# Reordering the first layer's projections, one exponential per group, and 64-column halves for the in-chunk products of a Mamba-2 + differential-attention trunk

## The chip, the cores and the metric

The kernel runs on one core of a Trainium2 chip, in one launch. A core has a matrix engine (TensorE, in the profile PE, with its weight loads apart as PEld), three engines for elementwise work (VectorE: DVE, ScalarE: ACT, GpSimd: POOL) and a queue engine (SyncE: SP) that starts transfers. Each engine takes its own instructions strictly in the order of its list and waits for the others by semaphores. The metric is the time of one execution on the device in microseconds (us); lower is better.

## The reference

Two layers over 512 tokens of width 1024. The first is a Mamba-2 layer with eight groups of four heads, the second differential attention against shared keys and values. Only the first layer is touched here:

```python
def ssd_chunked_scan(xdt, adt, bm, cm):
    def step(state, inp):
        x_c, a_c, b_c, c_c = inp
        acs = jnp.cumsum(a_c, axis=1)
        seg = acs[:, :, None] - acs[:, None, :]
        decay = jnp.exp(jnp.where(causal, seg, -jnp.inf))
        cb = jnp.einsum("blgn,bsgn->blsg", c_c, b_c)
        y_diag = jnp.einsum("blsgr,bsgrp->blgrp", cb[..., None] * decay, x_c)
        y_off = jnp.einsum("blgn,bgrpn->blgrp", c_c, state) * jnp.exp(acs)[..., None]
        to_end = jnp.exp(acs[:, -1:] - acs)
        new_state = (state * jnp.exp(acs[:, -1])[..., None, None]
                     + jnp.einsum("blgn,blgrp->bgrpn", b_c, x_c * to_end[..., None]))
        return new_state, y_diag + y_off
...
def mamba2_layer(x, ...):
    h = rms_norm(x, norm_g)
    zxbcdt = h @ w_in
    ...                                  # causal conv of width 4 and SiLU on x, B, C; softplus on dt
    y = ssd_chunked_scan(xs * dt[..., None], a * dt, bm, cm)
    y = y + d_skip.reshape(G, R, 1) * xs
    y = gated_group_rms_norm(y, z, gate_norm_g)   # y * silu(z), then RMS norm over each group's 256 channels
    return x + y @ w_out
```

After it come one shared key/value projection, the attention layer with its own projections, and a final RMS norm.

## The kernel before

All numbers are float32. Each weight matrix and each activation of a large product is split into a high part that the matrix engine multiplies at full speed and the low rest (`whi`/`wlo`, `a_hi`/`a_lo`, `yh`/`yl`); one product is then three matmuls (`mm3`, high-high, high-low, low-high). The small products of the scan are plain float32, and the matrix engine records two passes for each of them.

The first layer is cut into segments, each with two 1 MB weight blocks that are fetched and split ahead of use (ACT writes `whi`, DVE writes `wlo`; buffers for two blocks of each, so a block's `whi` can be written only when the block two before it has been multiplied for the last time):

- `z0` to `z3`: the gate projection for 512 channels, that is two groups; results leave PSUM through a SiLU on ACT (`z_out`, tile `zs`).
- `g0` to `g7`: a group's B, C and x columns (`pg`, 96 matmuls). Each of the four PSUM banks goes through the convolution (`conv`, tile `xc`): one multiply and three multiply-adds on DVE, two steps on ACT. The bank is free when the last multiply-add has read it.
- `o0` to `o3`: the output projection of two groups (`po`, 96 matmuls); DVE adds each bank to the residual `x_tok`. Segment `o3` needs `yh`/`yl` of groups 6 and 7; its second half is written apart (`last_rows`).

`order_a` sets the order of the segments. The projections form a stream (`stream_a`), and between them `ssd(g)` carries out the scan of group `g` in 128-token chunks: transposes (`pbt`, `pxt`), B·C products (`pcb`), dt-scaled x (`xdt`), the skip term (`dx`), states (`psA`, `psB`, `hst`), the in-chunk products (`pyd`: for each of four chunks and four heads, 128 weight columns of `dec` against 64 columns of `xdt`), the state's share (`po1`, `po2`, `tmp`), the gate, the group norm (`ss4`, `rsqrt`), and the transposition back (`pyt`) into `yh`/`yl`. Its tiles `xdt`, `dx`, `xe`, `hst` and `tmp` have one buffer each, so `ssd(g+1)` starts its `xdt` only when `ssd(g)` has read `dx` for the last time. `decays` fetches the cumulative decays (a broadcast DMA), subtracts and masks them on POOL and takes the exponentials on ACT. ACT loads a table each time it changes between SiLU and the exponential.

In this part the written order is not the order of execution on an engine. A scheduler that works ahead of time merges the stream and the scan into one fixed list for each engine. It chooses by its own estimate of times, and what it chose is seen below. From `last_rows` on the written order holds.

Of the kernel before, what the change touches and what calls it, by code (L numbers as in the profile page):

```python
# [17 lines left out]
P = 128  # L18
# [4 lines left out]
G = 8  # L23
R = 4
HD = 64
H = 32
NQ = 4
# [3 lines left out]
BIG = 1e30  # L31
# [6 lines left out]

C_GA, C_GK, C_GB, C_GG, C_SG, C_DTB, C_AL, C_CB, C_CW = 0, 8, 16, 24, 40, 41, 42, 43, 75
N_PAR = 203  # L40


class Ordered:
# [18 lines left out]
def trunk(ctx, tc, x, x_t, par, w_dt, w_in, w_out, w_kvqg, w_bo, d_skip, lam_qk, fin_g, out):  # L62
    nc = tc.nc
    V, A, T = (Ordered(tc, e) for e in (nc.vector, nc.scalar, nc.tensor))
    GP = nc.gpsimd
# [21 lines left out]

    order_a = "z0 g0 g1 z1 g2 g3 z2 g4 o0 g5 z3 g6 g7 o1 o2 o3".split()  # L90
    segs = []
    for it in order_a + ORDER_B:
        segs += [(it[0], int(it[1]) if len(it) == 2 else it, k) for k in range(2 if it[0] in "zgo" else 1)]
# [28 lines left out]
    def load(i):  # L122
# [8 lines left out]
        def split():  # L131

            pool, tags = (bp, ("dec", "dec")) if seg == ("o", 3, 1) else (wp, ("whi", "wlo"))
            hi, lo = (pool.tile([P, nk, w], F32R, tag=tag, name=f"{n}{i}", bufs=2) for n, tag in zip(("whi", "wlo"), tags))
# [207 lines left out]
    conv_out = {}  # L342

    def z_out(j, t, ps):
        zs = bp2.tile([P, 512], F32, tag="zs", name=f"zs{j}_{t}", bufs=6)
        A.activation(zs, ps, AF.Silu, scale=r_col[:, t:t + 1])
        zt[j, t] = zs

# [180 lines left out]
    bss = small.tile([P, 2, NT], F32, name="bss", bufs=1)  # L529
    decs = {}  # L530

    def decays(j):

        for g in (2 * j, 2 * j + 1):
            hs = slice(R * g, R * g + R)
            dec = bp.tile([P, R, NQ, P], F32, tag="dec", name=f"dec{g}", bufs=2)
            nc.sync.dma_start(dec.rearrange("p h c l -> p (h c l)"),
                                acs_d[hs].rearrange("h c l -> (h c l)").partition_broadcast(P))
            een = small.tile([P, R, 2], F32, tag="een", name=f"een{g}")
            GP.tensor_copy(een, dec[:, :, 1:3, P - 1])  # L540
            for h in range(R):
                GP.tensor_tensor(out=dec[:, h], in0=dec[:, h], in1=acs_tok[:, :, R * g + h].unsqueeze(2).to_broadcast([P, NQ, P]), op=ALU.subtract)
                GP.affine_select(out=dec[:, h], in_=dec[:, h], compare_op=ALU.is_ge, fill=-BIG, base=0,
                                 pattern=[[0, NQ], [1, P]], channel_multiplier=-1)
            decs[g] = (dec, een)
        for g in (2 * j, 2 * j + 1):
            dec, een = decs[g]
            A.activation(een, een, AF.Exp)
            for h in range(0, R, 2):
                A.activation(dec[:, h:h + 2], dec[:, h:h + 2], AF.Exp)  # L550

    def ssd(g):
        bc, cc, x0, x1 = conv_out.pop(g)
# [58 lines left out]
        T.matmul(po1[:, 256:512], lhsT=cc[:, P:2 * P], rhs=hsf[:, 0], start=True, stop=True)  # L612
# [1 line left out]
        for c in (2, 3):  # L614
# [5 lines left out]
        zo = (g % 2) * 256  # L620
        u = dx.rearrange("p c h e -> p c (h e)")
        tm = tmp.rearrange("p c h e -> p c (h e)")
        for c in range(NQ):
            if c:
                GP.tensor_tensor(out=u[:, c], in0=u[:, c], in1=tm[:, c], op=ALU.add)
            V.tensor_tensor(out=u[:, c], in0=u[:, c], in1=zt[g // 2, c][:, zo:zo + 256], op=ALU.mult)
# [492 lines left out]
```

## Time and profile before

| what | us |
|---|---|
| median of 3 runs | 737.5 (737.13 to 738.17) |
| the profiled execution's own time | 736.51 |
| its span, first to last instruction | 734.7 |
| PE busy, as the profile models it | 723.1 |
| PE weight loads (PEld) | 605.0 |
| DVE / ACT / POOL busy | 530.8 / 445.3 / 114.8 |
| ACT table loads, 33 of them | 42.3 |
| in-chunk products `pyd`, 256 passes, as records | 30.3 |

A row of a timeline in the next part reads: start in the span, duration of the run of like instructions, engine, line, operation, written tile <- read tiles, shape, count, and in brackets the engine's idle time before it and what ended it. Nearly all instructions of PE, DVE and ACT bear line 53, that of a helper, and are told apart by their tiles. A PE matmul record is longer than its share of the engine, because the next one starts before it ends: a record of 0.39 us is followed by the next 0.23 us after its start.

### The profile page before, as it was taken

What the parts mean: (1) busy time and instruction counts of PE and PEld (TensorE: products, weight loads), DVE (VectorE), ACT (ScalarE), POOL (GpSimd) and SP (SyncE); (2) the same over time, 40 slices, a digit from 0 to 9 for tenths busy, and PEclk for the clock granted to TensorE, in tenths of its full rate; (3) what the DMA queues carried; (4) which work ended last, traced back from release to release, by engine and by line L of the source; (5) the groups of instructions that cost most, each with busy time, mean ns of one, the idle gap of its engine ahead of it and who ended that gap; (6) DMA issues with size and microseconds to landing.
All of it is one profiled execution on the core that took longest, in us unless ns stands there. A gap on an engine that the chain in (4) does not pass through costs nothing.

```text
span 734.7 us, 10327 instructions
## 1 busy us (share of the span) xinstructions
PE 723.1 (98%) x3733; PEld 605.0 (82%) x3733; DVE 530.8 (72%) x1202; ACT 445.3 (61%) x975; POOL 114.8 (16%) x158
## 2 busy tenths in 40 slices
PE   9999999999999999999999999999999999999996
PEld 7788878888887888877888879888898898889874
DVE  5679955798568669469895655666757857785886
ACT  6849672864829356256433258766766766766566
POOL 0117231402233141150110201000000000000002
PEclk9999999999999999999999999999999999999999
DMA  8552313224132233132113220331221131122003
GB/s 314 215 193 97 128 45 116 78 95 172 59 114 65 108 115 116 58 116 102 71 58 114 87 86 8 115 115 58 65 109 57 58 116 58 58 80 93 29 1 114
DMA packets 12914, 70.83 MB, mean 96 GB/s; under 512 B 1728, under 2 KB 2496, under 8 KB 5312
## 3 DMA queue, kind: packets, MB, share of 16 engines
q1 hardware_dynamic: 12576, 69.90, 26.5%
q8 instruction: 29, 0.48, 0.3%
q10 hardware_dynamic: 288, 0.28, 0.1%
q14 instruction: 21, 0.17, 0.1%
HBM read 68.02 MB, written 2.16 MB: 96 GB/s over the span
## 4 chain that ended last, share of the span: by engine, by line
PE 86%; DVE 6%; ACT 5%; issue 1%; DMA 1%; POOL 0%; ACTq 0%; POOLq 0%; SPq 0%
PE pg L53 20%; PE po L53 13%; PE pz L53 10%; PE pt L53 7%; PE pv L53 6%; PE pq L53 6%; PE pk L53 6%; PE pyd L53 4%; PE pb L53 3%; PE sc L53 3%; PE pc L53 2%; DVE wlo L53 2%; ACT L53 1%; PE pyt L53 1%; PE pxt L53 1%
## 5 line engine op out<-in xcount | busy, mean ns | idle before, releaser
L53 DVE SCALAR_TENSOR_TENSOR wlo<-raw,prm,whi 128x512 fp32r<-128x512 f32 (+1 forms) x256 | 151.4, 640 | 49.6 <-ACT whi L53 49.2
L53 ACT ACTIVATE whi<-raw,prm 128x512 fp32r<-128x512 f32 (+1 forms) x256 | 137.1, 609 | 58.5 <-PE pz L53 12.4
L53 PE MATMUL pg<-a_hi,whi 128*128 128x512 f32 x256 | 102.4, 401 | 0.4 <-DVE xc L53 0.4
L53 PE MATMUL pg<-a_hi,wlo 128*128 128x512 f32 x256 | 102.7, 404 | 0.0
L53 PE MATMUL pg<-a_lo,whi 128*128 128x512 f32 x256 | 101.4, 397 | 0.0
L53 DVE SCALAR_TENSOR_TENSOR xc<-pg,prc,xc 128x511 f32<-128x511 f32 (+2 forms) x96 | 70.0, 743 | 4.4 <-ACT xc L53 3.6
L53 PEld LDWEIGHTS pg<-a_hi,whi 128*128 128x128 f32 x256 | 48.2, 188 | 11.4 <-issue 0.8
L53 PEld LDWEIGHTS pg<-a_hi,wlo 128*128 128x128 f32 x256 | 48.1, 188 | 11.0
L53 PEld LDWEIGHTS pg<-a_lo,whi 128*128 128x128 f32 x256 | 48.2, 188 | 10.8
L53 PE MATMUL po<-whi,yh 128*128 128x512 f32 x128 | 50.9, 400 | 0.7 <-ACT yh L53 0.6
L53 PE MATMUL po<-wlo,yh 128*128 128x512 f32 x128 | 50.9, 400 | 0.4 <-DVE wlo L53 0.4
L53 PE MATMUL pz<-wlo,a_hi 128*128 128x512 f32 x128 | 50.5, 401 | 0.0
L53 PE MATMUL pz<-whi,a_lo 128*128 128x512 f32 x128 | 50.1, 399 | 0.0
L53 PE MATMUL po<-whi,yl 128*128 128x512 f32 x128 | 49.9, 396 | 0.0
L53 PE MATMUL pz<-whi,a_hi 128*128 128x512 f32 x128 | 49.6, 400 | 0.0
L53 ACT ACT_TABLE_LOAD x33 | 42.3, 1283 | 9.5 <-DVE xc L53 7.9
L957 POOL TENSOR_TENSOR ot<-ot,fg 128x512 f32<-128x512 f32 x4 | 5.1, 1285 | 257.6 <-PE pc L53 256.4
L53 ACT ACTIVATE s<-s,mx 128x128 f32<-128x128 f32 (+3 forms) x64 | 35.6, 559 | 9.5 <-DVE mx L53 9.3
L580 POOL TENSOR_TENSOR xe<-xdt,tok 128x256 f32<-128x256 f32 x24 | 15.4, 672 | 152.5 <-DVE xdt L53 152.5
L53 DVE CUSTOM_DVE_ANT_0 s<-sc,bias 128x128 f32<-128x128 f32 (+3 forms) x64 | 29.4, 488 | 12.3 <-PE sc L53 11.9
L53 PE MATMUL pv<-whi,b_hi 128*128 128x256 f32 x128 | 36.6, 286 | 0.0
L53 ACT ACTIVATE tmp<-dx 128x256 f32<-128x256 f32 x32 | 13.1, 411 | 38.0 <-DVE dx L53 38.0
(244 smaller groups left out, 1749.1 us busy)
## 6 DMA issues: line engine op xcount, KB each, us to landing
raw<-in_w_in SPq DMA_DIRECT2D x23, 1024.0 KB, 4.9
raw<-in_w_kvqg SPq DMA_DIRECT2D x16, 1024.0 KB, 4.8
dec<-acs_d SPq DMA_DIRECT2D x8, 1024.0 KB, 4.8
raw<-in_w_out SPq DMA_DIRECT2D x8, 1024.0 KB, 4.7
raw<-in_w_bo SPq DMA_DIRECT2D x4, 1024.0 KB, 4.8
x_tok<-in_x SPq DMA_DIRECT2D x4, 512.0 KB, 9.4
out<-ot SPq DMA_DIRECT2D x7, 256.0 KB, 2.4
raw<-in_w_in SPq DMA_DIRECT2D x4, 256.0 KB, 5.4
```

The costliest lines, as they stand in the source:

```text
L53: i = op(*args, **kw)
L580: GP.tensor_tensor(out=xe[:, c], in0=xdt[:, c], in1=toe_tok[:, c, hs].unsqueeze(2).to_broadcast([P, R, HD]), op=ALU.mult)
L957: GP.tensor_tensor(out=o, in0=o, in1=f, op=ALU.mult)
```

## The change

Three things are changed.

1. `order_a`: `z0 g0 g1 z1 g2 g3 z2 g4 o0 g5 z3 g6 g7 o1 o2 o3` becomes `z0 g0 z1 g1 g2 z2 g3 o0 g4 z3 g5 o1 g6 g7 o2 o3`. To go with it, a gate tile is kept for each group (256 channels, 12 buffers) in place of one for two groups (512 channels, 6 buffers); its SiLU is two instructions in place of one.
2. `decays` is called for one group, two groups ahead, in place of two groups at once. The decays that `een` held lie behind `dec` in one tile of 2056 columns, and one exponential covers both in place of three.
3. Each product of `pyd` is done as two: weight columns 0 to 63 into PSUM partitions 0 to 63, and columns 64 to 127 into partitions 64 to 127.

```diff
+N_DEC = R * NQ * P + 2 * R
...
-    order_a = "z0 g0 g1 z1 g2 g3 z2 g4 o0 g5 z3 g6 g7 o1 o2 o3".split()
+    order_a = "z0 g0 z1 g1 g2 z2 g3 o0 g4 z3 g5 o1 g6 g7 o2 o3".split()
...
     def z_out(j, t, ps):
-        zs = bp2.tile([P, 512], F32, tag="zs", name=f"zs{j}_{t}", bufs=6)
-        A.activation(zs, ps, AF.Silu, scale=r_col[:, t:t + 1])
-        zt[j, t] = zs
+        for i in range(2):
+            zs = bp2.tile([P, 256], F32, tag="zs", name=f"zs{j}_{t}_{i}", bufs=12)
+            A.activation(zs, ps[:, i * 256:(i + 1) * 256], AF.Silu, scale=r_col[:, t:t + 1])
+            zt[2 * j + i, t] = zs
...
-    def decays(j):
-        for g in (2 * j, 2 * j + 1):
-            hs = slice(R * g, R * g + R)
-            dec = bp.tile([P, R, NQ, P], F32, tag="dec", name=f"dec{g}", bufs=2)
...
-        for g in (2 * j, 2 * j + 1):
-            dec, een = decs[g]
-            A.activation(een, een, AF.Exp)
-            for h in range(0, R, 2):
-                A.activation(dec[:, h:h + 2], dec[:, h:h + 2], AF.Exp)
+    def decays(g):
+        hs = slice(R * g, R * g + R)
+        both = bp.tile([P, N_DEC], F32, tag="dec", name=f"dec{g}", bufs=2)
+        dec = both[:, 0:R * NQ * P].rearrange("p (h c l) -> p h c l", h=R, c=NQ)
+        een = both[:, R * NQ * P:].rearrange("p (h q) -> p h q", h=R)
...
+        A.activation(both, both, AF.Exp)
+        decs[g] = (dec, een)
...
                     o = (c % 2) * 256 + h * HD
-                    T.matmul(pyd[q][:, o:o + HD], lhsT=dec[:, h, c, :], rhs=xdt[:, c, h, :], start=True, stop=True)
+                    for r in (slice(0, 64), slice(64, 128)):
+                        T.matmul(pyd[q][r, o:o + HD], lhsT=dec[:, h, c, r], rhs=xdt[:, c, h, :], start=True, stop=True)
...
-        if g % 2 and g < G - 1:
-            decays((g + 1) // 2)
+        if g < G - 2:
+            decays(g + 2)
...
     decays(0)
+    decays(1)
```

In `split`, the last block of `o3` borrows the two `dec` buffers; it now takes the first 2048 columns of the larger tile. `o3` and all that follows it are as before.

The lists that the scheduler makes of it differ from the first layer's beginning to its end. Three places count for the prediction. The first is PE at the end of the first layer, around the scan of group 7 (`pyd7`, `po17`, `po27`, `pyt7`) and the output projections `po2` and `po3`. Before, the second block of products stands inside `po2`, and 23 more matmuls of `po2` and the 24 of `po3` that need only group 6 follow ahead of `pyt7`:

```order
L53 MATMUL po2_1_1_3566<-whi29_3406,yl5_2664 128x512
L53 MATMUL po2_1_2_3580<-whi29_3406,yh4_2206 128x512
L53 MATMUL pyd7_1_3290<-xdt7_3243,dec7_2601 128x64 x8
L53 MATMUL po17_3300<-hst7_3267,xc31_3171 128x256
L53 MATMUL po27_3302<-hst7_3267,xc31_3171 128x256 x2
L53 MATMUL po2_1_2_3580<-wlo29_3407,yh4_2206 128x512
...
L53 MATMUL po3_0_3_3676<-whi30_3474,yl6_3068 128x512
L53 MATMUL pyt7_0_3338<-ident_74,tmp7_3279 128x128
...
L53 MATMUL po3_0_0_3628<-whi30_3474,yh7_3336 128x512
```

Now:

```order
L55 MATMUL po3_0_3_3812<-whi30_3474,yl6_3324 128x512
L55 MATMUL psA7_3524<-xe7_3515,bt7_3497 128x256 x2
L55 MATMUL psB7_3530<-xe7_3515,bt7_3497 128x256
L55 MATMUL pyd7_0_3536<-xdt7_3499,dec7_2840 64x64 x16
L55 MATMUL pyd7_1_3554<-xdt7_3499,dec7_2840 64x64 x16
L55 MATMUL po17_3572<-hst7_3523,xc31_3427 128x256
L55 MATMUL po27_3574<-hst7_3523,xc31_3427 128x256 x2
L55 MATMUL pyt7_0_3610<-ident_74,tmp7_3535 128x128
...
L55 MATMUL po3_0_0_3764<-whi30_3474,yh7_3608 128x512
```

What moved: all of `po2` and the part of `po3` that needs only group 6 now stand ahead of `psA7`; between `psA7` and `pyt7` no projection is left. The products are 64 by 64 and twice as many.

The second place is ACT just before that, between the scaling of group 6 (`tmp6`, the last reading of `dx6`) and the state of group 7. `whi32` is the first block of the next layer. It takes the buffer of `whi29`, which the last matmul of `po2` reads. Before:

```order
L53 ACTIVATE tmp6_3010<-dx6_2975,y_y_3051 128x256 x4
L53 CAST yh6_3067<-pyt6_0_3069 128x512
L53 CAST yh6_3067<-pyt6_1_3076 128x512
L53 COPY bt7_3241<-pbt7_3237 128x384
L53 ACTIVATE whi29_3406<-raw29_3404,prm_70 128x512 x4
L53 ACTIVATE whi31_3542<-raw31_3540,prm_70 128x512 x4
```

Now:

```order
L55 ACTIVATE tmp6_3250<-dx6_3215,y_y_3307 128x256 x4
L55 ACTIVATE whi32_3746<-raw32_3744,prm_70 128x256 x8
L55 COPY bt7_3497<-pbt7_3493 128x384
L55 CAST yh6_3323<-pyt6_0_3325 128x512
L55 CAST yh6_3323<-pyt6_1_3332 128x512
L55 COPY hst7_3523<-psA7_3524 128x256
```

What moved: the copies that PE waits for (`bt7` frees the bank of `pxt7_0`, `yh6` feeds `po3`) stand behind eight splits that wait for the end of `po2`.

The third is DVE where `o0` begins, which now follows `g3` directly. From the bank `pg3_3` to the first sums of `o0`, the list is now:

```order
L55 TENSOR_TENSOR pg3_3_1699<-pg3_3_1699,ar_row_263 128x512
L55 SCALAR_TENSOR_TENSOR xc6_1822<-pg3_2_1698,prc_72,xc6_1822 128x511
L55 TENSOR_SCALAR y_i_1545<-v42_1541 128x4
L55 SCALAR_TENSOR_TENSOR wlo15_1763<-raw15_1760,prm_70,whi15_1762 128x512
L55 TENSOR_TENSOR dec3_1195<-dec3_1195,pcb3_1864 128x512 x4
L55 SCALAR_TENSOR_TENSOR wlo15_1763<-raw15_1760,prm_70,whi15_1762 128x512
L55 SCALAR_TENSOR_TENSOR xc6_1822<-pg3_2_1698,prc_72,xc6_1822 128x510
L55 TENSOR_SCALAR y_y_1543<-y_i_1545 128x4
L55 SCALAR_TENSOR_TENSOR wlo15_1763<-raw15_1760,prm_70,whi15_1762 128x512 x2
L55 SCALAR_TENSOR_TENSOR xc7_1841<-pg3_3_1699,prc_72,xc7_1841 128x511
L55 TENSOR_TENSOR x_tok_73<-po0_0_0_1860,x_tok_73 128x512
L55 TENSOR_TENSOR x_tok_73<-po0_0_1_2030,x_tok_73 128x512
```

What moved: the sum that frees the bank of `po0_0_0` for `po0_0_2` stands behind eleven rows of convolution, splits and decays, while on PE 4 products of `pcb3` and 24 matmuls lie between the last of `pg3_3` and the first of `po0_0_2`. At `o1`, now directly behind `g5`, the list is of the same kind: `po1_0_1` waits for the sum of `po1_0_0`.

More of the change, by code (lines that the diff above doesn't have):

```diff
@@ L133, in split @@
             pool, tags = (bp, ("dec", "dec")) if seg == ("o", 3, 1) else (wp, ("whi", "wlo"))
-            hi, lo = (pool.tile([P, nk, w], F32R, tag=tag, name=f"{n}{i}", bufs=2) for n, tag in zip(("whi", "wlo"), tags))
+            if pool is bp:
+                hi, lo = (pool.tile([P, N_DEC], F32R, tag=tag, name=f"{n}{i}", bufs=2)[:, 0:2048].rearrange("p (k n) -> p k n", k=nk)
+                          for n, tag in zip(("whi", "wlo"), tags))
+            else:
+                hi, lo = (pool.tile([P, nk, w], F32R, tag=tag, name=f"{n}{i}", bufs=2) for n, tag in zip(("whi", "wlo"), tags))
             ready[seg] = (hi, lo)
@@ L530, in trunk @@
     decs = {}
-    def decays(j):
-        for g in (2 * j, 2 * j + 1):
-            hs = slice(R * g, R * g + R)
-            dec = bp.tile([P, R, NQ, P], F32, tag="dec", name=f"dec{g}", bufs=2)
[L537 to L545, printed above, removed]
-        for g in (2 * j, 2 * j + 1):
-            dec, een = decs[g]
-            A.activation(een, een, AF.Exp)
-            for h in range(0, R, 2):
-                A.activation(dec[:, h:h + 2], dec[:, h:h + 2], AF.Exp)
+    def decays(g):
[3 more added lines that the diff above has]
+        een = both[:, R * NQ * P:].rearrange("p (h q) -> p h q", h=R)
+        nc.sync.dma_start(both[:, 0:R * NQ * P],
+                            acs_d[hs].rearrange("h c l -> (h c l)").partition_broadcast(P))
+        GP.tensor_copy(een, dec[:, :, 1:3, P - 1])
+        for h in range(R):
+            GP.tensor_tensor(out=dec[:, h], in0=dec[:, h], in1=acs_tok[:, :, R * g + h].unsqueeze(2).to_broadcast([P, NQ, P]), op=ALU.subtract)
+            GP.affine_select(out=dec[:, h], in_=dec[:, h], compare_op=ALU.is_ge, fill=-BIG, base=0,
+                             pattern=[[0, NQ], [1, P]], channel_multiplier=-1)
+        A.activation(both, both, AF.Exp)
+        decs[g] = (dec, een)
     def ssd(g):
@@ L619, in ssd @@
                         in1=eacs_tok[:, 2:4, hs].unsqueeze(3).to_broadcast([P, 2, R, HD]), op=ALU.mult)
-        zo = (g % 2) * 256
         u = dx.rearrange("p c h e -> p c (h e)")
@@ L625, in ssd @@
                 GP.tensor_tensor(out=u[:, c], in0=u[:, c], in1=tm[:, c], op=ALU.add)
-            V.tensor_tensor(out=u[:, c], in0=u[:, c], in1=zt[g // 2, c][:, zo:zo + 256], op=ALU.mult)
+            V.tensor_tensor(out=u[:, c], in0=u[:, c], in1=zt[g, c], op=ALU.mult)
             A.activation(tm[:, c], u[:, c], AF.Square, accum_out=ss4[:, c:c + 1])
```

## The prediction

> **What bounds the kernel now.** I read the page's engine times first, then the chain of waits, then who waits for whom on PE.
>
> ```profile
> span 734.7 us, 10327 instructions
> PE 723.1 (98%) x3733; PEld 605.0 (82%) x3733; DVE 530.8 (72%) x1202; ACT 445.3 (61%) x975; POOL 114.8 (16%) x158
> PE 86%; DVE 6%; ACT 5%; issue 1%; DMA 1%; POOL 0%; ACTq 0%; POOLq 0%; SPq 0%
> ```
>
> PE is busy for 98% of the span and carries 86% of the chain that ended last. So a change pays in two ways only: PE gets less to do, or it waits less. How much it waits stands in the next rows, PE's waits over the whole kernel.
>
> ```profile
> PE pyt L53 <- ACT tmp L53: 1.0, 2, 0.7
> PE po L53 <- ACT yh L53: 0.6, 1, 0.6
> PE po L53 <- DVE wlo L53: 0.4, 1, 0.4
> PE pg L53 <- DVE xc L53: 0.4, 1, 0.4
> ```
>
> These four groups, 2.4 us, are all of the first layer but the start. The rows count from the modelled end of a matmul, which lies later than the moment the next could start. The pace comes from the first and last of 19 projection matmuls in a row:
>
> ```profile
> 409.92 0.39 PE L53 MATMUL po<-whi,yh 128*128 128x512 f32 x1
> 414.09 0.40 PE L53 MATMUL po<-whi,yh 128*128 128x512 f32 x1
> 414.34 1.89 PE L53 MATMUL pyd<-xdt,dec 128*128 128x64 f32 x16
> 416.06 1.51 PE L53 MATMUL po<-hst,xc 128*128 128x256 f32 x6
> ```
>
> 4.17/18 is 0.232 us a matmul against a record of 0.39, so each wait hides 0.16 more: 5 x 0.16 + 2.4 = 3.2 us. The first layer has little waiting to win back, and new waits would be added in full.
>
> **The products.** By the two last rows, 16 passes take 416.06 - 414.34 = 1.72 us, 0.1075 each; the 256 of the kernel take 27.5 us. What sets that pace?
>
> ```profile
> L53 PE MATMUL pyd<-xdt,dec x256: 217/275/275, 76.7 to 416.0; 128*128 128x64 f32 x128
> L53 PEld LDWEIGHTS pyd<-xdt,dec x256: 187/192/192, 76.5 to 415.9; 128*128 128x128 f32 x128
> ```
>
> A pass moves only 64 columns and has one load of 128 weight columns. The changed kernel has 512 passes with 64 weight columns each. No row shows such a pass, so I bound it. Lower end: half the load time (0.054) and the two halves beside each other in their own columns of the array, 512 x 0.054 / 2 = 13.75 us. Middle: half the load time one after the other, 27.5. Upper end: a pass costs 0.1075 whatever its width, 55. I take the lower end, because load and output of the two halves share no column, and add a price for changing shape: PE may have to run dry where 64-column passes begin and end. That costs at most what a record outlasts its pace, 0.275 - 0.1075 = 0.167. The new order has 15 runs of products, 30 changes, 0 to 5.0 us; I take 5.0. Term: -13.75 + 5.0 = **-8.75**, bounds -13.75 and +32.5.
>
> The Trainium skill bears on both choices. "TensorE: Matmul & The Clock Gate", section "LDWEIGHTS (loading the stationary operand)", has the load's time go with its columns at 1.2 per ns, 0.107 for 128; the 0.1075 agrees. "TensorEngine Tiling (Array Packing)", section "Key Properties", says that tiles load and multiply in parallel, but also that "Changing tiling mode (not just tile) drains the TensorE"; the first alone would make the term -13.75, the second is a rule against the change, and no run here shows either.
>
> **The end of the layer.** The order of the changed kernel puts nothing on PE between `psA7` and `pyt7` but the scan itself. Before, 47 projection matmuls covered it. These rows carry that chain from the products to the first `po` that reads group 7:
>
> ```profile
> 416.87 2.73 DVE L53 SCALAR_TENSOR_TENSOR wlo<-raw,prm,whi 128x512 fp32r<-128x512 f32 x4
> 419.52 1.01 DVE L53 TENSOR_TENSOR tmp<-po,tok 128x256 f32<-128x256 f32 x2
> 420.02 2.32 POOL L625 TENSOR_TENSOR dx<-dx,tmp 128x256 f32<-128x256 f32 x3 [9.19 <-DVE tmp L53]
> 421.05 1.90 DVE L53 TENSOR_TENSOR dx<-dx,zs 128x256 f32<-128x256 f32 x3
> 422.97 0.19 ACT L53 ACTIVATION_READ_ACCUMULATOR tmp<-dx 128x1 f32 x1
> 423.87 0.40 ACT L53 ACTIVATE tmp<-dx 128x256 f32<-128x256 f32 x1
> 424.26 2.50 ACT L53 ACTIVATE whi<-raw,prm 128x256 fp32r<-128x256 f32 x6
> 424.40 0.17 DVE L53 TENSOR_SCALAR v<-ss 128x4 f32<-128x4 f32 x1
> 427.66 0.16 DVE L53 TENSOR_TENSOR y_c<-y_y,v 128x4 f32<-128x4 f32 x1
> 428.05 0.17 DVE L53 SCALAR_TENSOR_TENSOR y_y<-y_c,y_y 128x4 f32<-128x4 f32 x1
> 428.10 0.39 PE L53 MATMUL po<-whi,yl 128*128 128x512 f32 x1
> 428.88 1.64 PE L53 MATMUL pyt<-ident,tmp 128*128 128x128 f32 x8 [0.39 <-ACT tmp L53]
> 431.08 0.50 PE L53 MATMUL po<-whi,yh 128*128 128x512 f32 x1 [0.57 <-ACT yh L53]
> ```
>
> From the last product (416.06) to `pyt` (428.88) are 12.8 us. Two things in it go, because the next layer's splits now come earlier. The root from 424.40 to 428.22 (3.8 us) is ten small operations that alternate with splits; unmixed they follow each other at 0.195 (427.66, two further, 428.05), 1.95 us, so 1.9 less. The last square starts at 423.87 behind two splits and could at 423.16: 0.6 less, rounding down. The four `wlo` at 416.87, which can only be written when the products have left the `dec` buffers, stay ahead of `tmp` as they are. So 10.3 us from products to `pyt`, and 2.2 (428.88 to 431.08) to `po`. PE's own work in these 12.5 us is priced by four rows, each run by the start of the next:
>
> ```profile
> 391.75 1.04 PE L53 MATMUL pyt<-ident,tmp 128*128 128x128 f32 x8
> 392.62 0.49 PE L53 MATMUL pbt<-ident,xc 128*128 128x128 f32 x3
> ...
> 407.24 0.59 PE L53 MATMUL psB<-xe,bt 128*128 128x256 f32 x2
> 407.67 1.89 PE L53 MATMUL pyd<-xdt,dec 128*128 128x64 f32 x16
> ```
>
> `po17`/`po27`, six passes at 0.215, are 1.3 and `pyt`, eight transposes at 0.109, 0.87: PE is idle for 10.3.
>
> Ahead of it, ACT's list has `whi32` before `bt7` and `yh6`, and `whi32` waits for the last matmul of `po2`; call its end 0. Group 6's transposition is then done and queued behind that wait are two copies PE needs. The costs:
>
> ```profile
> 393.57 0.49 ACT L53 COPY bt<-pbt 128x384 f32<-128x384 f32 x1
> 430.44 1.07 ACT L53 CAST yh<-pyt 128x512 fp32r<-128x512 f32 x2 [0.42 <-PE pyt L53]
> 398.93 0.69 DVE L53 TENSOR_TENSOR xdt<-pxt,tok 128x512 f32<-128x512 f32 x1 [0.57 <-PE pxt L53]
> 400.90 1.76 POOL L580 TENSOR_TENSOR xe<-xdt,tok 128x256 f32<-128x256 f32 x3 [26.42 <-DVE xdt L53]
> ```
>
> Eight splits (0.417 each by the row with six) end at 3.5, `bt7` at 4.0, the first `yh6` at 4.5. `pxt7_0` runs from 4.05; the first 8 matmuls of `po3` from 4.55 to 6.4; `pxt7_1` to 6.85, the other 16 to 10.6. DVE has `yl6`, `xdt7` and `dx7` in between, about 0.65 each, the last `xdt7` done near 7.7; `xe7` ends near 9.5, in time. Then `psA7`/`psB7` 1.3 and the products at their old price 3.45: end 15.3. PE's own work in that is 0.87 + 0.33 + 0.87 + 5.6 + 1.3 + 3.45 = 12.4, so 2.9 idle. Together 13.2 us. Before, the same stretch idles from 428.10 + 0.23 to 428.88 and for 431.08 - 428.88 - 0.87: 1.9 us. Term: **+11.3**. Bounds: +7 if the copies come without the 2.9 and the chain is 1.5 shorter; +14 if DVE is behind.
>
> **The middle.** At `o0` PE reaches `po0_0_2` 4 x 0.22 + 24 x 0.232 = 6.5 us after the last of `pg3_3`. DVE's list to the sum that frees the bank:
>
> ```profile
> 232.74 1.88 DVE L53 TENSOR_TENSOR dec<-dec,pcb 128x512 f32<-128x512 f32 x3
> 234.53 2.85 DVE L53 SCALAR_TENSOR_TENSOR wlo<-raw,prm,whi 128x512 fp32r<-128x512 f32 x4
> 213.42 1.52 DVE L53 SCALAR_TENSOR_TENSOR xc<-pg,prc,xc 128x511 f32<-128x511 f32 x2
> ```
>
> Four `dec` at 0.6, four `wlo` at 0.7, three `xc` at 0.7, the bank's multiply and the sum at 0.6, two small ones at 0.2: 8.9, with 0.2 of hand-over (a matmul's record outlasts its pace by 0.16) 9.1, so 2.6 idle. At `o1` the same count from the last of `pg5_1` to `po1_0_1` (36 matmuls and three transposes, 8.7) against 17 DVE rows at about 0.65 and hand-over (11.3) gives 2.6. Against these stand the waits of before that the new list needn't have (`xc`, `wlo` and one `pyt`, 0.4 + 0.4 + 0.65 + 3 x 0.16 = 1.9), of which I expect half again: by a count of matmuls `pyt0` and `pyt4` now get 12.9 us of cover after their products, and `pyt7` had 12.2 before and waited. Term: 5.2 - 1.9 + 0.9, **+4**, bounds -2 (all old waits gone, DVE ahead) and +8.
>
> **Exponentials, table loads and gates** change ACT alone:
>
> ```profile
> L53 ACT ACT_TABLE_LOAD x33 | 42.3, 1283 | 9.5 <-DVE xc L53 7.9
> L53 ACT ACTIVATE dec<-dec 128x1024 f32<-128x1024 f32 x16 | 16.6, 1055 | 1.1 <-POOL dec L543 1.0
> L53 ACT ACTIVATE zs<-pz,ar_col 128x512 f32<-128x512 f32 x16 | 10.6, 678 | 1.4 <-PE pz L53 1.3
> ```
>
> The new list has 23 table loads, 10 x 1.28 = 12.8 us less; the exponentials cost about the same, the halved gates some 3 more. ACT is busy for 445 of 735 us, so 0; what it shortens of PE's waits is in the middle's lower bound. The DMAs of `dec` are the same eight; each now waits on SP for one group's products instead of two groups', and two weight blocks stay in flight ahead: 0.
>
> **The sum**, against the profiled execution's own time: 736.5 - 8.75 + 11.3 + 4 = 743.05. That execution lies 1.0 below the median of the runs, so 744.
>
> **The rivals.** (a) The halves don't run beside each other: the products stay at 27.5 plus changes of shape, term +5: 757.8, and 753 without the changes. For it: nothing in the trace shows two loads at once; at 55 us it would be near 785, which I count here as a tail. (b) The other side, faster: PE changes shape for nothing and DVE keeps ahead in the middle, 737.5 - 13.75 + 11.3 - 2 = 733. One mechanism, products in half the time with nothing handed back; it decides when changes and middle together cost under 2.45. For it: 12.8 us of table loads less in a stage whose waits end at ACT and DVE. Against: DVE's list at `o0` holds nothing of what ACT saves. (c) A draw, 736 to 739: the end is 7 rather than 11.3. That the products stay whole is ruled out by the list (64x64, 16 a bank).
>
> **Chances.** Forecast 0.45; (a) 0.28; (b) 0.17; (c) 0.10. The likeliest's own range is 740 to 750; for 8 in 10 I reach to (b)'s 733 and (a)'s 758. A difference of 0.2% (1.5 us) is about what a measurement can tell: faster 0.17, same 0.10, slower 0.73.
>
> **What would show it.** A wait of PE's `pyt` for ACT `tmp` of 8 to 10 us, once, at the layer's end, and `pxt` or `po` waiting for ACT's copies about 3; `po` waiting for DVE `x_tok` twice in the middle; `pyd` at a pass each 0.027 (right), 0.054 (rival a) or 0.1075. Wrong would be a `pyt` wait under 5 us.

## The result, and the profile after

The changed kernel takes 761.19 us (median of 4 runs, 759.10 to 765.33) against 737.44 (4 runs, 737.13 to 738.17). The ratio is 1.0327, 95% interval 1.0283 to 1.0372. It is 23.75 us slower. The forecast was 744 with a range of 733 to 758, so the direction was right, the size was not, and the time lies above the range.

The first rows of the changed kernel's page, and its chain:

```profile
span 759.4 us, 10828 instructions
PE 723.9 (95%) x3989; PEld 599.5 (79%) x3989; DVE 538.7 (71%) x1202; ACT 432.9 (57%) x965; POOL 115.8 (15%) x158
PE 81%; DVE 11%; ACT 4%; issue 2%; DMA 1%; POOL 1%; POOLq 0%; ACTq 0%; SPq 0%; DVEq 0%
```

PE falls from 98% to 95% of the span: it now waits. DVE's share of the chain that ended last grows from 6% to 11%. The view of the waits says for what PE waits (total in us, times, longest); by its rows ACT ends 14.5 us of it and DVE 11.6:

```profile
PE po L55 <- DVE x_tok L55: 10.2, 2, 5.5
PE pyt L55 <- ACT tmp L55: 8.6, 1, 8.6
PE pxt L55 <- ACT bt L55: 2.6, 1, 2.6
PE pbt L55 <- ACT xc L55: 1.8, 1, 1.8
PE pg L55 <- DVE xc L55: 1.1, 1, 1.1
PE pz L55 <- ACT whi L55: 1.0, 1, 1.0
PE po L55 <- ACT yh L55: 0.5, 1, 0.5
PE pg L55 <- DVE wlo L55: 0.3, 1, 0.3
```

These are 26.1 us in nine waits of the first layer. With the 0.16 that each hides it is 27.5, against 3.2 before. The products, the same view of one tile as before (duration min/median/max in ns, first and last start):

```profile
L55 PE MATMUL pyd<-xdt,dec x512: 222/222/270, 82.0 to 442.3; 128*64 128x64 f32 x171
```

512 passes on half the columns (128*64), as the list had it. The waits alone are 24.3 us more than before and the products are cheaper, so something else must have been lost. It stands in the granted clock. The windows view of the changed kernel, in two stretches around a wait (PE busy, in brackets its instructions, then the granted clock, DMA share and GB/s):

```profile
198.31:201.72 3.41, 1.53 (x7) 1.00 0.30 127
201.72:205.13 3.41, 0.00 (x0) 1.00 0.18 19
205.13:208.54 3.41, 3.22 (x8) 0.50 0.70 288
...
444.06:447.47 3.41, 0.00 (x0) 1.00 0.17 24
447.47:450.88 3.41, 0.00 (x0) 0.50 0.69 283
450.88:454.29 3.41, 1.73 (x8) 0.50 0.00 0
454.29:457.71 3.42, 2.96 (x8) 0.50 0.01 2
457.71:461.12 3.41, 3.41 (x16) 1.00 0.00 0
```

After the wait at `o0` PE works for 3.4 us at half clock: 8 matmuls in place of 16. After the wait at the layer's end it is the same until 457.71. Five such stretches stand in the changed kernel (from 205.1, 259.7, 321.2, 430.4 and 447.5), eight windows of 3.41 us in all, each stretch behind a wait; before, there is none until the last 3 us of the span. PE is busy in them for about 20 us, of which half is lost, less about 1 us in which the transposition of group 7 follows ACT's pace anyway: 9 us, an estimate from these views.

The three together, -8 (products, below) + 24.3 + 9 = 25.3, stand against a first layer that ends 25.3 us later (the next layer's first transposition starts at 470.58, before at 445.30). What follows it is as long as before to within 0.6 us.

### The profile page after: what moved, and what is told of

The parts are those of the page before. It is cut to its first block, busy times and chain, and to the rows that moved or that the text cites. A ratio compares the mean times of both kernels' runs of the same rounds, so it can differ in the third digit from the quotient of the medians.

```text
span 759.4 us, 10828 instructions
## 1 busy us (share of the span) xinstructions
PE 723.9 (95%) x3989; PEld 599.5 (79%) x3989; DVE 538.7 (71%) x1202; ACT 432.9 (57%) x965; POOL 115.8 (15%) x158
## 4 chain that ended last, share of the span: by engine, by line
PE 81%; DVE 11%; ACT 4%; issue 2%; DMA 1%; POOL 1%; POOLq 0%; ACTq 0%; SPq 0%; DVEq 0%
PE po L55 15%; PE pg L55 14%; PE pz L55 12%; PE pt L55 7%; PE pq L55 6%; PE pv L55 6%; PE pk L55 6%; DVE wlo L55 4%; PE pb L55 3%; PE sc L55 3%; PE pyd L55 2%; PE pc L55 2%; DVE xc L55 1%; PE pxt L55 1%; DMA dec<-acs_d 1%
## 5 line engine op out<-in xcount | busy, mean ns | idle before, releaser
L55 PE MATMUL po<-whi,yh 128*128 128x512 f32 x128 | 54.1, 426 | 10.7 <-DVE x_tok L55 10.2
L55 PE MATMUL po<-wlo,yh 128*128 128x512 f32 x128 | 53.2, 417 | 0.0
L55 PE MATMUL pz<-whi,a_hi 128*128 128x512 f32 x128 | 51.5, 417 | 1.0 <-ACT whi L55 1.0
L55 ACT ACTIVATE xc<-pg,prc 128x512 f32<-128x512 f32 x32 | 24.5, 772 | 27.9 <-DVE pg L55 25.9
L55 PEld LDWEIGHTS po<-whi,yh 128*128 128x128 f32 x128 | 25.8, 202 | 18.1 <-DVE x_tok L55 11.6
```

The source lines that it names most:

```text
L55: i = op(*args, **kw)
```

## The experiments

The merge into lists is remade at every edit, so an edit that is undone also moves hundreds of other rows. The first three runs let that happen. Most of the later ones hold every engine's list to a given one, row by row, by edges of order without any wait:

```diff
+    def follow(self, text):
...
+        for a, b in zip(seq, seq[1:]):
+            self.tc.add_manual_dep(b.ins, a.ins.name, how, reason="row order")
...
+    T.follow(ROWS_T)
+    V.follow(ROWS_V)
+    A.follow(ROWS_A)
```

The tables `ROWS_` are the lists of before or of the changed kernel as numbers; GpSimd's and SyncE's are held in the same way.

**Halves alone, lists remade.**

```diff
-                    T.matmul(pyd[q][:, o:o + HD], lhsT=dec[:, h, c, :], rhs=xdt[:, c, h, :], start=True, stop=True)
+                    for r in (slice(0, 64), slice(64, 128)):
+                        T.matmul(pyd[q][r, o:o + HD], lhsT=dec[:, h, c, r], rhs=xdt[:, c, h, :], start=True, stop=True)
```

> The kernel before with one edit: each in-chunk product as two column halves. Theory (costs add): in the changed kernel a run of 16 products took 1.43 us from the start of the matmul ahead to the next full-pace matmul, against 1.87 to 1.90 before; 16 runs give 7.2 us, so 737.4 - 7.2 = 730.2. Rival (in this order DVE and ACT set the pace and a faster product only turns into a wait of PE): 735 to 738, with a longer wait of pyt for ACT. Second rival (halves cost more where they stand between projections): above 738.

Measured: 744.62 us, ratio 1.0099 (1.0082 to 1.0116). All three theories are off the mark as they were put; it is slower, but not at the products. Its longest wait:

```profile
PE po L53 <- DVE x_tok L53: 6.8, 1, 6.8
```

A wait of 6.8 at `o0` is new, with half clock behind it. It comes with the remade list: the fifth run, the same edit in the lists of before, does not have it. So this run says nothing yet of what halves cost.

**The new order alone, lists remade.** The order of the segments and the gate tiles per group, nothing else.

```diff
-    order_a = "z0 g0 g1 z1 g2 g3 z2 g4 o0 g5 z3 g6 g7 o1 o2 o3".split()
+    order_a = "z0 g0 z1 g1 g2 z2 g3 o0 g4 z3 g5 o1 g6 g7 o2 o3".split()
```

> The kernel before with the new order of the segments and the gate tiles per group alone; decays for two groups at once with three exponentials, products whole. Theory (the order makes the waits): the waits of the changed kernel, 24 us, and the half clock behind them, 8 to 9 us, appear without the other two parts, so 737.4 + 33 = 768 to 771, with a pyt wait of 8 us at the end of the layer. Rival (the decays per group, whose POOL work stands beside DVE's at the sums of o0 and o1, make the waits in the middle): only the end's 11 and its 3 of half clock come, 750 to 753.

Measured: 758.19 us, ratio 1.0275 (1.0258 to 1.0293), between the two theories.

```profile
PE pyt L53 <- ACT tmp L53: 8.8, 2, 8.6
PE po L53 <- DVE x_tok L53: 6.7, 2, 6.2
```

The end's wait of `pyt` is there in full without the other two parts, and so is one at `o0`; the other wait for `x_tok` is 0.5 in place of 4.7, and the 2.6 of `pxt` is not there. The wait of `pyt` belongs to the order. For the others the list that was made of it decides.

**Products whole again, lists remade.**

```diff
-                    for r in (slice(0, 64), slice(64, 128)):
-                        T.matmul(pyd[q][r, o:o + HD], lhsT=dec[:, h, c, r], rhs=xdt[:, c, h, :], start=True, stop=True)
+                    T.matmul(pyd[q][:, o:o + HD], lhsT=dec[:, h, c, :], rhs=xdt[:, c, h, :], start=True, stop=True)
```

> The changed kernel with one edit undone: products whole again. Theory (costs add): 761.2 + 7.2 = 768.4. Rival (longer products cover part of what PE waits for, so the waits shrink): 763 to 766.

Measured: 752.73 us, ratio 1.0207 (1.0192 to 1.0223). That is 8.5 faster than the changed kernel, outside both theories. The wait of `pyt` is 8.6 as ever; those for `x_tok` are no longer among its long ones. Again another list, not another price of the products.

**Something for PE to do while it waits.** Only one row is added, on PE, behind `po27`; all other rows stand where they stood.

```diff
+        if g == G - 1:
+            hot = long_bank("hot")
+            for i in range(72):
+                T.transpose(hot[:, 0:P], hsf[:, 2, 0:P], ident)
```

> The changed kernel with 72 transposes of the last state put on PE into a spare bank where PE waits 8.75 us for the root of group 7; no other row of any list moves. They take 72 x 0.109 = 7.85 us, less than the wait. Theory (the granted clock falls to 0.5 because PE stands still for some microseconds): the clock stays at 1.0 through the transposition and the first po of group 7, which then run at 0.109 and 0.233 in place of 0.22 and 0.43, and the kernel is 2 us faster, 759. Rival (the clock falls for another reason, at a set time or by load): granted clock 0.5 there as before, and the time stays at 761 or grows by what 72 transposes at half pace, 15.7 us, exceed the wait, to 768.

Measured: 762.92 us, ratio 1.0343 (1.0327 to 1.0358), where the theory had 759. The windows view:

```profile
446.06:449.47 3.41, 3.41 (x33) 1.00 0.35 79
449.47:452.88 3.41, 3.41 (x33) 1.00 0.55 233
452.88:456.30 3.42, 2.11 (x11) 1.00 0.00 0
456.30:459.71 3.41, 3.41 (x9) 0.50 0.01 2
```

The clock now stays at 1.00 through the wait, but falls one window later. In that window PE still waited 0.74 for `tmp` and 0.57 for `yh`, and its eight transposes followed ACT's four scalings at 0.43 a pair, of which PE needs 0.22: by starts and paces it stood idle for a share of 0.68 of this window (the busy column counts records, which run on into a gap). As put, the theory missed; its condition had to be made sharper, which the tenth run does.

**Halves in the lists of before.** This is the first experiment again with the lists held.

```diff
                     for r in (slice(0, 64), slice(64, 128)):
+                        T.join = r.start > 0
                         T.matmul(pyd[q][r, o:o + HD], lhsT=dec[:, h, c, r], rhs=xdt[:, c, h, :], start=True, stop=True)
```

(`join` makes two halves count as one row of the table.)

> The kernel before with each product as two halves, and every engine's list held to that of before row by row (the scheduler had remade the lists when the halves were put in alone, and that kernel took 744.6). Theory (the halves are faster in themselves, the remade lists cost the time): a run of products is 0.45 us shorter, 16 runs give 7.2, so 737.8 - 7.2 = 730.6, with no wait at o0 above 1 us. Rival (halves cost on PE itself what they save, at the changes of shape or in the loads around them): 737 to 745. A middle result (some of the gain turns into PE waiting for ACT and DVE): 732 to 735.

Measured: 729.95 us (729.78 to 730.50), ratio 0.9899 (0.9882 to 0.9917): 7.7 us faster than before, where 7.2 were expected, and faster than both kernels. One run of products in its timeline:

```profile
407.98 0.40 PE L153 MATMUL po<-whi,yh 128*128 128x512 f32 x1
408.30 1.15 PE L153 MATMUL pyd<-xdt,dec 128*64 128x64 f32 x32
409.38 1.56 PE L153 MATMUL po<-hst,xc 128*128 128x256 f32 x6
```

Its longest waits in the layer:

```profile
PE pyt L153 <- ACT tmp L153: 1.2, 3, 0.6
PE po L153 <- DVE wlo L153: 1.0, 1, 1.0
```

From the matmul ahead (407.98) to the first behind (409.38) are 1.40 us. Before, at the same place, it was 416.06 - 414.09 = 1.97. The first matmul behind lasts 0.05 longer now, so a run is about 0.5 shorter, 8 us for 16, a little more than the 0.45 of the expectation. The halves do pay, by nearly what they were worth in the sum. What the first run lost was the list's.

**Whole products in the lists of the changed kernel.** The third experiment again, lists held.

```diff
-                    for r in (slice(0, 64), slice(64, 128)):
-                        T.matmul(pyd[q][r, o:o + HD], lhsT=dec[:, h, c, r], rhs=xdt[:, c, h, :], start=True, stop=True)
+                    T.matmul(pyd[q][:, o:o + HD], lhsT=dec[:, h, c, :], rhs=xdt[:, c, h, :], start=True, stop=True)
...
+    T.follow(ROWS_T)
```

> The changed kernel with the products whole, and every engine's list held to that of the changed kernel. Theory (costs add): 761.2 + 7.2 = 768.4, the waits as they were. Rival (the longer products cover part of the waits at pbt, o0, o1): 763 to 766. The opposite, faster than 761, would speak for halves that cost on PE itself.

Measured: 771.40 us (769.73 to 773.98), ratio 1.0462 (1.0433 to 1.0491): 10.2 slower than the changed kernel. The waits are as they were (`x_tok` 10.5, `pyt` 8.6, `pxt` 2.6 in its list), so nothing is covered by the longer products; the 3 us beyond the expected 768.4 lie within the spread of this and of the changed kernel (4 and 6 us).

**POOL writes in place of reading.** For group 4 alone, whose subtraction and mask POOL carries out while DVE nears the sums of `o0`. They are left out, so that group 4's decays are constants.

```diff
+            if g == 4:
+                GP.memset(dec[:, h], -1.0)
+                GP.memset(dec[:, h], -0.5)
+                continue
```

> The changed kernel, lists held, with POOL's subtraction and mask of group 4's decays (eight instructions, from 191.8 to 200.0 in the changed kernel) replaced by eight memsets of the same tiles; group 4's decays are then constants. Theory (a DVE instruction that runs beside POOL's subtraction is held until POOL is done: wlo 1.2 in place of 0.65, v and y_i 1.0 and 0.43 in place of 0.17; memsets, which read nothing, hold nobody): DVE reaches the sum of po0_0_0 3 us earlier, the wait at o0 falls from 5.6 to 2.6, the half clock behind it shrinks or goes, and the kernel takes 756 to 758. Rival (DVE is late for another reason, ACT's whi or its own list): the wait stays at 5 to 6 and the time at 761.

First the changed kernel's timeline there, of DVE and below of POOL:

```profile
191.00 0.69 DVE L55 TENSOR_TENSOR pg<-pg,ar_row 128x512 f32<-128x512 f32 x1
191.60 3.66 DVE L55 SCALAR_TENSOR_TENSOR wlo<-raw,prm,whi 128x512 fp32r<-128x512 f32 x3
195.18 1.01 DVE L55 TENSOR_SCALAR v<-ss 128x4 f32<-128x4 f32 x1
196.71 0.73 DVE L55 SCALAR_TENSOR_TENSOR xc<-pg,prc,xc 128x511 f32<-128x511 f32 x1
204.59 1.28 DVE L55 TENSOR_TENSOR x_tok<-po,x_tok 128x512 f32<-128x512 f32 x2
...
191.81 5.37 POOL L550 TENSOR_TENSOR dec<-dec,tok 128x512 f32<-128x512 f32 x4
197.13 2.85 POOL L551 TENSOR_SCALAR_AFFINE_SELECT dec<-dec 128x512 f32<-128x512 f32 x4
```

Then with the memsets:

```profile
191.47 2.07 DVE L155 SCALAR_TENSOR_TENSOR wlo<-raw,prm,whi 128x512 fp32r<-128x512 f32 x3
193.45 0.16 DVE L155 TENSOR_SCALAR v<-ss 128x4 f32<-128x4 f32 x1
201.28 1.28 DVE L155 TENSOR_TENSOR x_tok<-po,x_tok 128x512 f32<-128x512 f32 x2
...
189.72 3.80 POOL L155 MEMSET dec<- 128x512 f32 x8
```

And its waits for the sums:

```profile
PE po L155 <- DVE x_tok L155: 5.6, 2, 3.3
```

And the window in which the wait at `o0` ends:

```profile
201.58:204.99 3.41, 2.97 (x13) 1.00 0.95 308
```

Measured: 757.60 us (756.77 to 761.18), ratio 1.0282 (1.0251 to 1.0313). The three `wlo` from 191.60 take 3.66 together (two of them 1.5 each) where POOL subtracts, and 2.07 beside the memsets, which last until 193.5. `v` on 128x4 takes 1.01 in place of 0.16; it and the rows behind it now run when POOL is done. Rows that read one operand from PSUM (`pg`, `xc`) take 0.69 and 0.73 in both. The sum starts 3.3 us earlier, the wait at `o0` is 2.3 by its row and 2.5 with what it hides, and the clock stays at 1.00 behind it. The theory holds, with the 2.6 that the prediction had for this wait. The other of the two waits, 3.3, is at `o1`, where it was 4.7; the part on the prediction comes back to it.

**Three sums moved forward on DVE.** Only DVE's table differs from the changed kernel's, in the places of `x_tok` for `po0_0_0`, `po0_0_1` and `po1_0_0`:

```diff
 SCALAR_TENSOR_TENSOR wlo15<-raw15,prm,whi15 128x512
+TENSOR_TENSOR x_tok<-po0_0_0,x_tok 128x512
 TENSOR_TENSOR dec3<-dec3,pcb3 128x512 x4
+TENSOR_TENSOR x_tok<-po0_0_1,x_tok 128x512
...
 SCALAR_TENSOR_TENSOR xc7<-pg3_3,prc,xc7 128x511
-TENSOR_TENSOR x_tok<-po0_0_0,x_tok 128x512
-TENSOR_TENSOR x_tok<-po0_0_1,x_tok 128x512
```

> The changed kernel, lists held but for three rows of DVE: the sum of po0_0_0 moved ahead of group 3's four dec products, that of po0_0_1 right behind them, that of po1_0_0 right behind the multiply of bank pg5_3. Theory (these waits of PE are rows on DVE that stand in the wrong place): both x_tok waits go but for about 1 us, 9.5 us, and with them the half clock behind each, 3 us, so 748 to 750. Rival (DVE is behind as a whole, and what it does later makes PE wait elsewhere): under 4 us gained, 757 to 761, with new waits for xc, wlo or x_tok.

Measured: 753.65 us (752.02 to 754.88), ratio 1.0217 (1.0195 to 1.0239): 7.5 faster than the changed kernel, where 11 to 13 were expected and under 4 by the rival.

```profile
PE pyt L155 <- ACT tmp L155: 9.5, 2, 8.6
PE po L155 <- DVE xc L155: 1.6, 1, 1.6
PE po L155 <- DVE y_c L155: 1.1, 1, 1.1
PE po L155 <- DVE x_tok L155: 0.8, 1, 0.8
```

The two long waits and the two half clocks behind them are gone; 3.6 us of it (1.6, 1.1 and 0.9 more of `pyt`) come back as waits for what DVE does later. A row's place was most of these two waits, DVE being behind the rest. Part of the gain is luck: two more windows of half clock are gone, one behind `pxt` and one near 260, though `pxt` still waits 2.6 and `pbt` 1.8.

**Rows moved at the layer's end.** On ACT `bt7` and both `yh6` ahead of the eight `whi32`; on DVE the eight `wlo32` behind group 7's `xdt` and `dx`, and four `wlo31` behind group 7's root.

```diff
 ACTIVATE tmp6<-dx6,y_y 128x256 x4
-ACTIVATE whi32<-raw32,prm 128x256 x8
 COPY bt7<-pbt7 128x384
 CAST yh6<-pyt6_0 128x512
 CAST yh6<-pyt6_1 128x512
+ACTIVATE whi32<-raw32,prm 128x256 x8
```

> The changed kernel, lists held but for the layer's end: on ACT the copies bt7 and yh6 ahead of the eight whi32 splits; on DVE the eight wlo32 behind group 7's xdt and dx, and the four wlo31 behind group 7's root. Theory (the end's waits are rows that stand in the wrong place, as the sum of the prediction has it): the wait of pxt, 2.7, goes and with it the half clock behind it, 1.6; the four wlo31 no longer stand ahead of tmp7, so the wait of pyt falls from 8.7 to 6.0; 761.2 - 7.0 = 754. Rival (what is moved back is itself late next): PE waits for wlo31 or wlo32 instead and the time stays above 758.

Measured: 756.10 us (755.74 to 757.14), ratio 1.0255 (1.0240 to 1.0271).

```profile
PE po L155 <- DVE x_tok L155: 10.3, 2, 5.5
PE pyt L155 <- ACT tmp L155: 6.2, 1, 6.2
PE pbt L155 <- ACT xc L155: 2.3, 1, 2.3
```

The wait of `pxt` and the half clock behind it are gone, that of `pyt` is 6.2 for the 6.0 expected: 5.1 us less in all of the 7.0. The theory of these waits holds. What is left of the end, 6.2, is the scan of group 7 with nothing on PE beside it.

**PE kept at work through the end.** As the fourth run, with 92 transposes in place of 72, also between and behind the pairs of `pyt`.

```diff
+        fill_pe(80)
...
                 T.transpose(pyt[:, c * P:(c + 1) * P], tm[:, c, j * P:(j + 1) * P], ident)
+                if j:
+                    fill_pe(2 if c < 3 else 6)
```

> The changed kernel, lists held, with 92 transposes of the last state into a spare bank on PE: 80 while it waits for the root of group 7, two behind each of the first three pairs of pyt and six behind the last, so that PE stands still for less than a third of any 3.4 us there. Theory (the clock is set once in 3.41 us, and halves for the next 3.41 after a stretch in which PE stood idle for some two thirds or more): no 0.5 between 440 and 470, the first po of group 7 at 0.233 in place of 0.43, and 1 to 2 us less in all, 759 to 761. Rival (the clock falls by a count of work or for another reason there, as with the 72 transposes, where it fell at 456.3): 0.5 appears again near 456 and the time is 761 to 763.

The windows view behind the wait:

```profile
449.81:453.22 3.41, 3.41 (x30) 1.00 0.00 0
453.22:456.63 3.41, 3.41 (x16) 1.00 0.01 2
```

No half clock from 432.7 to the last microseconds, and 16 matmuls in the window where the changed kernel had 8 (454.29 to 457.71). That part of the theory holds and its rival falls. The time does not bear it out: 763.32 (5 runs, 758.32 to 763.79; the views are of the fastest), ratio 1.0354 (1.0337 to 1.0371), where 759 to 761 were expected. The filling work ends the wait no earlier, and the two waits for `x_tok` are 8.3 here in place of 10.2; what the other runs lost was not looked into.

**Decays per group and one exponential alone, lists remade.**

```diff
-            A.activation(een, een, AF.Exp)
-            for h in range(0, R, 2):
-                A.activation(dec[:, h:h + 2], dec[:, h:h + 2], AF.Exp)
+        A.activation(both, both, AF.Exp)
...
-        if g % 2 and g < G - 1:
-            decays((g + 1) // 2)
+        if g < G - 2:
+            decays(g + 2)
```

> The kernel before with the second part alone: decays per group, two groups ahead, one exponential for each; order and whole products as before. The scheduler remakes the lists (99 of 3070 rows of PE differ). Theory (ACT's table loads and exponentials are off the path, and POOL's work per group comes at other times but is no more): 736 to 739. Rival (POOL's work of one group now falls beside DVE's rows that PE waits for): 740 to 745. Opposite rival (a fifth of ACT's table loads less shortens the waits that end at ACT): 733 to 736.

Measured: 736.40 us (735.90 to 737.39), ratio 0.9990 (0.9980 to 0.9999): no difference of note, as the first theory has it.

**Rows moved in the fastest kernel.** The fifth run's kernel with rows moved at `o0` and at the layer's end, as the expectation lists them. Of DVE's and ACT's tables at the end, word for word:

```diff
-SCALAR_TENSOR_TENSOR wlo31<-raw31,prm,whi31 128x512 x4
...
-ACTIVATE whi32<-raw32,prm 128x256 x2
...
 CAST yh7<-pyt7_1 128x512
+ACTIVATE whi32<-raw32,prm 128x256 x8
```

> The kernel before with the halves and its own lists (729.95), and rows moved where PE still waits: at the layer's end DVE's wlo31 and wlo32 behind group 7's root, ACT's whi32 behind yh7, six matmuls of po3 that need only group 6 from ahead of pyt7 to behind it; at o0 ACT's scaling of group 3 (tmp3) ahead of two whi17 splits, and DVE's first wlo16 four rows earlier. Theory (each of these waits is a row in the wrong place): pyt7's 0.48 and the 0.73 for yh7 go, the 0.8 of pyt3 goes, 0.7 of the 1.2 at wlo16 goes: 2.7 less, 727.2. Rival (the rows put back are late next): 729 to 732.

Measured: 733.97 us (10 runs, 731.38 to 737.40), ratio 0.9956 (0.9937 to 0.9975): 4 us slower than with the rows left alone. The rival's mechanism decides, with more than its price (the view is of a run of 736.32):

```profile
PE po L153 <- DVE x_tok L153: 2.7, 1, 2.7
PE po L153 <- DVE yl L153: 2.1, 1, 2.1
```

`tmp3` ahead of two `whi17` made `wlo17` late (DVE waits 1.5 for ACT), and the sum behind it on DVE with it; half clock follows. At the end `yl7` stood behind twelve splits that now waited for the moved `whi32`. Four waits of 0.5 to 1.2 were given for two of 2 to 3 and some below 1.

## Why the prediction was right or wrong

| step of the prediction | predicted | measured | from |
|---|---|---|---|
| the products | -8.75 | -7.7 | fifth run; -8 by the starts in the traces |
| the end of the layer | +11.3 | +10.9 | waits of `pyt`, `pxt`, `yh`: 8.6 + 2.6 + 0.5 + 3 x 0.16, less 1.3 before |
| the middle | +4 | +13.5 | six other waits: 14.4 + 6 x 0.16, less 1.9 before |
| exponentials, table loads, gates | 0 | -0.7, ratio 0.9990 | eleventh run (without the gates) |
| half clock behind waits | not in the sum | +9, an estimate | windows view |

**The products** were right in mechanism and nearly in size. The halves run beside each other: two start 0.007 us apart and the next pair follows 0.051 later, 0.058 for what took 0.1075. The change of shape costs, too, a little less than the 5.0 taken: the matmul ahead of a run lasts 0.09 longer, the run itself 0.15 more than its sixteen pairs, the first matmul behind it up to 0.05 more than before, 0.29 in each of 15 runs, 4.4. The Trainium skill's page "TensorEngine Tiling (Array Packing)", section "Key Properties", states both halves of this (tiles work in parallel; a change of mode drains the engine); the trace agrees with the first, 0.058 a pair, and shows for the second that a change has a price, 0.29 a run, though not what PE does in it. Rival (a), the halves one after the other, falls, and so does the whole width at the old price.

**The end** was right: `pyt` and the `yh` behind it waited 8.6 and 0.5 for 10.3 of idling, `pxt` 2.6 for 2.9, and rows of ACT and DVE moved there did what the step says of them (ninth run). The sign named for it, a wait of `pyt` of 8 to 10 once and one of about 3 at `pxt`, was there.

**The middle** is the first step that failed, by 9.5 us. The two waits named, at `o0` and `o1`, did come, and for the rows named, but were 5.5 and 4.7 in place of 2.6 each. At `o0` the rows of DVE were counted rightly, each at its undisturbed length and from the moment `pg3_3` is there. But six DVE instructions between 191.6 and 198.9 (three `wlo`, `v`, `y_i` and another `wlo`) stand beside POOL's subtraction and mask of group 4; five of them are longer, by 3.2 us in all, so DVE came to those rows late. With POOL's reading taken away the wait was 2.5. The prediction said nothing of POOL's work beside DVE's, and the trace of before had it: all its 38 DVE instructions that last over 0.15 us longer than the median of their kind stand beside an instruction of POOL, 17 us in all; the changed kernel has 41, 24 us. The Trainium skill's page "SBUF — State Buffer", section "Who interferes with whom", states the rule: a VectorE instruction with two inputs in SBUF and a GpSimd instruction that reads SBUF hold each other up, and a GpSimd instruction that only writes does not. The rows of `wlo` agree, held beside the subtraction and not beside the memsets, and so do `pg` and `xc`, which read one operand from PSUM and are not held. `v` and `y_i` read one tile alone and were held too; the rule as put does not cover them, and no run here isolates what holds them.

At `o1` the record shows a longer way from the same hold. First the changed kernel, then the seventh run:

```profile
303.36 1.71 ACT L55 ACTIVATE tmp<-dx,y_y 128x256 f32<-128x256 f32 x4 [3.31 <-DVE y_y L55]
309.95 1.29 DVE L55 TENSOR_TENSOR yl<-pyt,yh 128x512 fp32r<-128x512 f32 x2 [1.60 <-ACT yh L55]
305.09 1.29 DVE L155 TENSOR_TENSOR yl<-pyt,yh 128x512 fp32r<-128x512 f32 x2 [0.24 <-ACT yh L155]
```

In the changed kernel four steps of a group's root, from 299.3 to 303.3, take 0.90 to 0.98 beside POOL's next subtraction. ACT waits for that root, its copy `yh` comes late, and DVE stands 1.60 us for `yh` ahead of the rows that lead to the sum. In the seventh run only two steps were held, DVE stood 0.24, and the wait at `o1` was 1.4 shorter. The prediction counted these rows without a wait among them. This is read from two traces; no run tested it alone.

The rest of the middle, 4.2 us of waits for `xc`, `whi` and `wlo` at 256 to 260, 373 and 115, was booked at half of the old waits, 0.9. DVE's rows ahead of the first stand beside POOL as well (two `wlo` of 1.6 and two `y_c` of 1.0 from 244 to 249). None was tested by a run of its own. So of the 9.5 about 3 us, at `o0`, have a cause shown by a run; about 2, at `o1`, one read from traces; and about 4, in these waits, stay open.

**Half clock** is the second step that failed: it is missing. The sum added waits and took the work behind them at 0.232 a matmul. In the trace of before no wait ahead of the kernel's last microseconds is long enough to show it. A rule of the Trainium skill names it and was not weighed: "TensorE: Matmul & The Clock Gate", section "Part 1: The HAM clock gate", has the clock fall to half after an idle window of about 3.4 us and come back after a busy one. Of the waits as the prediction sized them (2.9, 10.3 and twice 2.6) only the 10.3 is as long as that window; the runs show that shorter ones count too, 2.6 at `pxt`. The prediction cited this page for the weight loads and left out the section that spoke against its own waits.

With the two, 743 + 9.5 + 9, less 0.4 of the end and plus 1.0 of the products, is 762 for the profiled execution, where 761.5 was measured. That the sum closes rests in part on the estimate of 9. **Rival (b)**, faster by halves that cost nothing, needed the middle at -2; it was +13. Its first half, however, is the fifth run: where the lists do not change, the halves make the kernel 1.0% faster. **Rival (c)** fell with the end at its full size. The chances had 0.73 on slower, which it is; the range was too narrow since both bounds of the middle came from rows that were not held by POOL, and none of its ends contained the clock.

## What to carry to other kernels

Where a scheduler makes the lists, an edit is two changes, the work and the lists, and they must be run apart: the same halves were worth -7.7 us in the old lists and +6.8 in lists remade for them. A new wait of PE is to be booked with what comes behind it (here another 1.7 us for each 3.4 us at half clock), and a row of DVE with two operands in SBUF at the length it has beside POOL, where POOL works at that time. A projection that could cover the next group's scan is worth more late than early: the end's 8.6 us came with the order alone, in all three lists that the scheduler made of it (the changed kernel, the second and the third run).

## What the runs showed of the hardware that was not expected

The granted clock is set anew every 3.41 us: all its steps in the fourteen traces of this study lie on a grid of that length. For each window of that grid at full clock, up to 700 us, PE's idle time was worked out from the starts of its matmuls and the pace of each kind. Of 34 windows with an idle share of 0.65 or more every one was followed by half clock; of more than 2700 clearly below 0.60 none; of the few near 0.60, one. So a wait of 2.6 us can be enough, at `pxt` for example, and one of 2.5 at `o0` was not (seventh run); for waits of that length their place on the grid decides. The eighth run shows it on one and the same wait: `pxt` waits 2.6 there as in the changed kernel, but across two windows, neither idle for more than 0.56 of its length, and no half clock follows. The changed kernel's runs, 759.1 to 765.3, spread over 6 us and those of the fifth run's kernel, which has no half clock, over 0.7; that the grid's place makes the difference is likely, and was not tested.

The hold of DVE by POOL costs a small instruction as much as a large one: `v` on 128x4 took 1.01 us in place of 0.16 and ended at 196.19, 0.03 behind the POOL instruction that it stood beside. The root of a group's norm is ten such steps of 0.2, and four of them, from 299 to 303 us of the changed kernel, took 0.90 to 0.98 each.
